# Splitting the normed input into two tiles, so that the last gate frees half of it in its middle and the attention output is loaded there

## The chip, the cores and the metric

The kernel runs on one core of one Trainium2 chip. It is written as one program of instructions for five engines (TensorE, VectorE, ScalarE, GpSimdE and SyncE; in the profile PE, DVE, ACT, POOL and SP), which wait for each other through semaphores. The metric is the device time of one launch in microseconds (us), median over runs. PEld is the weight load of PE, and SPq is SP's queue of transfers.

## The reference

One layer of a trunk with two branches over 640 tokens: 512 noisy tokens of one request and 128 context tokens. In short:

```python
h = _rmsnorm(x, p["norm1_g"]) * (1.0 + sc1) + sh1
u_rw, u_na, gate_rw, gate_na = jnp.split(h @ p["w_in"], IN_SPLITS, axis=-1)
o_rw, s_new = _rwkv_branch(u_rw, s0, ...)      # 8 heads, a scan forward and one backward
q, k, v = jnp.split(u_na, 3, axis=-1)          # 8 heads of attention in a 2-D neighbourhood
o_na = _na_latent(q, k, v, ctx_k, ctx_v, p["na_rpb"])
merged = (jax.nn.sigmoid(gate_rw) * (o_rw @ p["w_o_rwkv"])
          + jax.nn.sigmoid(gate_na) * (o_na @ p["w_o_na"]))
x = x + g1 * (merged @ p["w_out"])
h2 = _rmsnorm(x, p["norm2_g"]) * (1.0 + sc2) + sh2
x = x + g2 * ((jax.nn.silu(h2 @ p["ffn_w1"]) * (h2 @ p["ffn_w3"])) @ p["ffn_w2"])
```

d_model is 1024, each branch is 512 wide, the hidden layer of the feed-forward is 2816 wide. All is float32.

## The kernel before

**Two halves of every float32.** A matmul operand x is held as hi (x rounded to the type that PE multiplies at full rate) and lo (x minus hi). A product is three matmuls: hi by hi, hi by lo and lo by hi. The normed input h is held so, features on partitions: two tiles of 128 partitions by 8 feature blocks by 640 tokens (`hh` and `hl`, made by `hilo`, L314). `o`, the output of both branches, goes over the same two buffers once h is no longer read: `hilo("o")` asks for the same tags, and so each load of `o` waits for the last matmul that read the old content.

**The stages.** First the norm and q, k, v; then the attention, block by block; then four rounds (ct = 0 to 3, two heads each) of the other branch; then `w_out`, the second norm and the feed-forward. In a round, `inv` inverts 32 by 32 triangular blocks by a substitution in 30 steps on DVE (products into `pr`, L1249, and sums into `RL`, L1253), `carry` runs the chunked scan, `out` (L1385) normalises the round's result. In `inv`, three jobs of small matmuls (`v_job`, `t_job`, `g_job`: L1172, L1195, L1144, L1147, L1184) are issued after steps 2, 11 and 16 of the last round, and their results are masked on DVE after steps 4, 13 and 19 (L1156, L1159). The `out` of the round before runs beside `inv`; its matmuls are L1064, L1078 (five transposes) and L1407 (the gate, in two halves), and its DVE work L1398, L1399, L1402 and L1409 (two halves).

**The fill.** Between these instructions stands other dense work of PE, in the order of `PRM["order"]`: projections (k, r, v, l), sixteen gate blocks g0 to g15 (`gate_gen`, L534: sigmoid(gate) as a tanh, 24 matmuls for the first 320 tokens, a tanh on ACT, then 24 for the other 320, each result stored to `tna_d` or `trw_d`), and from a0 on the products of `o` with the output weights (`merge_gen`, L1450: a0 to a7 read o's blocks 0 to 3, the attention output; b0 to b7 read 4 to 6). g14 is the last gate, and a0 follows it. `flps` gives the fill two PSUM banks (`fl`) in turn.

**What sets the order.** PE, POOL, DVE and ACT execute in the order in which the code is written. `PRM["plan"]` gives for each step of the current stage how many matmuls of the fill, how many steps of `out` and how many of `bonus` (L1093, L1095) are written there. `later` puts an evacuation some steps behind its matmul. SP's transfers stand in an order of the scheduler's. `o_load(0, 6)` (L768) is written at the end of g14: twelve transfers of 320 KB, hi and lo of o's blocks 0 to 5; block 6 comes later.

Of the kernel before, what the change touches and what calls it, by code (L numbers as in the profile page):

```python
# [26 lines left out]
PRM = dict(  # L27
    order=("l0 l1 k0 r0 v0 l2 g0 g1 g2 k1 g3 r1 g4 g5 v1 g6 g7 k2 r2 g8 g9 v2 g10 g11 k3 r3 g12 g13 v3 g15 g14 a0 a1 a2 a3 a4 a5 a6 a7 "
     "b0 b1 b2 b4 b3 b5 b6 b7"),
    plan=(  # L30
        "22.0 0.0 2.0 4.0",
        ("0.0.0 2.0.0 2.0.1 10.0.0 2.0.0 2.0.1 2.0.1 2.0.1 2.0.1 2.0.1 10.0.0 2.0.0 2.0.0 10.0.0 2.0.0 2.0.0 "
         "2.0.0 10.0.0 2.0.0 2.0.0 2.0.0 2.0.0 2.0.0 2.0.0 2.0.0 2.0.0 2.0.0 2.0.0 2.0.0 2.0.0 5.0.0 24.0.0 "
         "20.0.0 10.0.0 8.0.0 8.0.0 0.0.0"),
        ("10.0 1.0 12.1 0.2 0.0 8.1 6.2 0.0 8.1 6.2 0.0 8.1 12.2 0.0 8.1 6.2 0.0 8.1 6.2 0.0 7.1 5.2 0.0 9.1 "
         "6.2 6.0"),
        "22.0 2.0 2.0 2.0",
        ("0.0.0 0.0.0 2.0.1 10.0.0 1.0.0 2.1.1 2.1.1 2.1.1 2.1.1 1.1.1 10.0.0 3.0.0 2.0.0 2.0.0 2.1.0 2.1.0 "
         "2.0.0 10.0.0 2.0.0 2.1.0 2.1.0 2.1.0 2.1.0 2.1.0 12.1.0 2.1.0 2.1.0 2.1.0 2.0.0 2.1.0 5.0.0 24.0.0 "
         "20.0.0 10.0.0 8.0.0 8.0.0 0.0.0"),  # L40
        ("10.0 0.0 8.1 6.2 0.0 8.1 6.2 0.0 8.1 6.2 0.0 8.1 6.2 0.0 8.1 6.2 0.0 7.1 6.2 0.0 8.1 6.2 0.0 8.1 "
         "6.2 6.0"),
        "22.0 2.0 0.0 5.0",
        ("0.0.0 10.0.0 2.0.1 10.0.0 2.0.0 2.1.1 2.1.1 2.1.2 2.1.1 2.1.0 10.0.0 2.0.0 2.0.0 2.0.0 2.1.0 2.1.0 "
         "2.0.0 10.0.0 2.0.0 2.1.0 2.1.0 3.1.0 4.1.0 2.1.0 2.1.0 2.1.0 2.1.0 4.1.0 2.1.0 2.0.0 5.0.0 24.0.0 "
         "18.0.0 8.0.0 9.0.0 8.0.0 0.0.0"),
        ("10.0 0.0 8.1 14.2 0.0 8.1 6.2 0.0 8.1 6.2 0.0 0.1 6.2 0.0 8.1 6.2 0.0 8.1 6.2 0.0 8.1 6.2 0.0 8.1 "
         "6.2 6.0"),
        "22.2 0.0 4.0 6.0",
        ("0.0.0 16.1.0 8.1.1 9.0.0 2.1.0 8.1.1 8.1.1 8.1.1 8.1.1 0.1.1 0.1.0 0.0.0 0.1.0 0.1.0 0.1.0 0.1.0 "  # L50
         "6.1.0 7.1.0 6.1.0 6.0.0 6.0.0 6.0.0 0.0.0 6.0.0 6.0.0 7.0.0 6.0.0 6.0.0 6.0.0 6.0.0 6.0.0 6.0.0 "
         "11.0.0 8.0.0 8.0.0 2.0.0 0.0.0"),
        ("10.0 0.0 8.1 6.2 0.0 8.1 4.2 0.0 8.1 6.2 0.0 8.1 6.2 0.0 8.1 6.2 0.0 8.1 6.2 0.0 8.1 6.2 0.0 8.1 "
         "14.2 6.0"),
        "2 0 6 6 6 4 4 5 2 0 5 1 1 0 0"),
    qp=((0, 0, 7, 6, 7), (2, 5, 4, 4, 3, 2, 5, 3, 1)), ada=2, pa=1, pd=0,
    lw=(0, 0, 0, 0, 0, 2, 2, 2, 2, 2, 2, 2, 2, 2, 2, 2),
# [50 lines left out]
def body(ctx: ExitStack, tc: tile.TileContext, xs, xp, cols, consts, w_ada, b_row, w_rw, w_qkv,  # L108
# [425 lines left out]
    def gate_gen(i, w, ps_, gsb, gtag):  # L534
        dst = trw_d[i] if i < 8 else tna_d[i - 8]
        for (a, b) in ((0, H2), (H2, NT)):
            t = gsb.tile([P, H2 if gtag == "fl" else 643], F32, tag=gtag, bufs=2, name=nm(gtag))[:, :H2]
            ps = ps_()
            yield from feat_gen(ps, w, (hh, hl), 8, a, b)

            def rest(t=t, ps=ps, a=a, b=b):
                act.activation(t, ps[:, :H2], AF.Tanh, scale=0.5)
                sp.dma_start(dst[:, a:b], t)
# [489 lines left out]
    with ExitStack() as s3:  # L1033
# [393 lines left out]
        def o_load(a, b):  # L1427

            if not o:
                o.extend(hilo("o"))  # L1430
            for q in range(a, b):
                for t, t_d in zip(o, o_d):
                    sp.dma_start(t.bitcast(F32)[:, q, :], t_d[q])
# [562 lines left out]
```

## Time and profile before

| what | us |
|---|---|
| median of 3 runs | 1203.76 |
| lowest and highest run | 1202.25 and 1204.63 |
| the profiled execution | 1201.55 |
| its span, first to last instruction | 1199.8 |
| PE busy in the span | 1128.0 |
| DVE busy in the span | 793.3 |
| ACT busy in the span | 503.6 |
| POOL busy in the span | 273.8 |

A row of a timeline gives the start in us from the span's start, the length in us, engine, line, operation, output <- inputs, shapes, a count, and in brackets the idle time of the engine ahead of it with what ended it. A row of the waits gives who waited <- for whom, us in total, times, and the longest. A row of the windows gives the stretch, its length, then for PE, PEld, DVE, ACT and POOL the busy time with the count, the granted PE clock as a share of full speed, the busy share of the DMA engines and GB/s.

### The profile page before, as it was taken

Reading aid. Unit: us, or ns where it says so; the run is one execution under the profiler, and the core shown is the slowest. Engines: PE = TensorE matmul, PEld = TensorE weight load, DVE = VectorE, ACT = ScalarE, POOL = GpSimd, SP = SyncE. Lnnn points to the kernel's source line nnn. Section 1 sums busy time; section 2 is a strip of 40 time slices with the busy share of each in tenths; the row PEclk is TensorE's granted clock in tenths of the full one; section 3 lists DMA queues with packets and bytes.
Section 4 is the critical chain, followed back from the end, with each engine's and each line's share of the span. In section 5 each row is a group of like instructions: output and inputs, shape, how many; then the busy total and the mean of one; then the engine's idle time right before and its main releaser. Section 6 shows DMA issues by size and latency. Waiting matters only on the chain.

```text
span 1199.8 us, 26920 instructions
## 1 busy us (share of the span) xinstructions
PE 1128.0 (94%) x11160; PEld 999.2 (83%) x11160; DVE 793.3 (66%) x1630; ACT 503.6 (42%) x1016; POOL 273.8 (23%) x354
## 2 busy tenths in 40 slices
PE   6999999998998899899789989989999999999998
PEld 4588877788887788788778878889889989998997
DVE  4565455569558838946594684888568756875675
ACT  4444666653454364346323331754224412442240
POOL 1162244343224323342231360200001000000000
PEclk9999999999899999999899989999999999999999
DMA  9752777531211221120432571312312231222122
GB/s 336 245 115 88 238 219 231 197 124 48 66 48 37 83 69 49 54 87 29 164 129 87 177 272 54 105 36 89 106 53 88 89 105 53 89 90 90 67 73 104
DMA packets 56578, 134.48 MB, mean 112 GB/s; under 512 B 7140, under 2 KB 22116, under 8 KB 56456
## 3 DMA queue, kind: packets, MB, share of 16 engines
q1 hardware_dynamic: 55592, 131.56, 33.1%
q8 instruction: 88, 1.44, 0.5%
q10 hardware_dynamic: 864, 1.20, 0.3%
q14 instruction: 34, 0.28, 0.1%
HBM read 118.41 MB, written 14.32 MB: 111 GB/s over the span
## 4 chain that ended last, share of the span: by engine, by line
PE 61%; DVE 11%; issue 2%; ACT 2%; DMA 1%; SPq 0%; POOL 0%; DVEq 0%; ACTq 0%
PE f L1715 23%; PE acc L283 16%; PE fl L196 10%; DVE pr L1249 2%; DVE RL L1253 2%; PE w L1361 1%; PE w L1321 1%; DVE AG L1104 1%; PE w L1333 1%; PE w L1348 1%; PE mm L196 1%; PE w L1147 1%; DMA tr<-trw_d 1%; PE w L1378 1%; DVE f L1262 1%
## 5 line engine op out<-in xcount | busy, mean ns | idle before, releaser
L196 PE MATMUL fl<-h,whi 128*128 128x320 f32 x704 | 170.4, 323 | 1.9 <-ACT U L515 1.0
L175 POOL TENSOR_TENSOR wlo<-wst,whi 128x256 fp32r<-128x256 f32 x118 | 102.8, 899 | 192.1 <-ACT whi L170 188.7
L1715 PE MATMUL f<-t,whi 128*128 128x320 f32 x640 | 141.4, 309 | 0.0
L1715 PE MATMUL f<-b,whi 128*128 128x320 f32 x608 | 136.4, 312 | 3.6 <-ACT b L185 1.8
L283 PE MATMUL acc<-whi,u 128*128 128x512 f32 (+1 forms) x448 | 135.9, 385 | 0.0
L196 PEld LDWEIGHTS fl<-h,whi 128*128 128x128 f32 x704 | 121.1, 192 | 6.8 <-ACT U L515 1.2
L170 ACT CAST whi<-wst 128x1024 fp32r<-128x1024 f32 (+2 forms) x86 | 81.8, 956 | 83.2 <-PE acc L283 32.9
L196 PE MATMUL fl<-h,wlo 128*128 128x320 f32 x352 | 114.6, 326 | 0.0
L1715 PEld LDWEIGHTS f<-t,whi 128*128 128x128 f32 x640 | 107.0, 188 | 0.0
L1715 PEld LDWEIGHTS f<-b,whi 128*128 128x128 f32 x608 | 102.8, 190 | 4.7 <-ACT b L185 2.2
L1770 POOL TENSOR_TENSOR ws<-wst 128x512 f32<-128x512 f32 x20 | 27.4, 1372 | 342.0 <-DVE wlo L1759 226.2
L1715 PE MATMUL f<-t,wlo 128*128 128x320 f32 x320 | 98.9, 309 | 0.0
L283 PEld LDWEIGHTS acc<-whi,u 128*128 128x128 f32 x448 | 83.5, 188 | 16.6
L1715 PE MATMUL f<-b,wlo 128*128 128x320 f32 x304 | 94.6, 311 | 1.4 <-DVE wlo L1759 1.4
L1756 ACT CAST whi<-ws 128x1024 fp32r<-128x1024 f32 x40 | 42.0, 1050 | 108.7 <-PE f L1715 48.5
L283 PE MATMUL acc<-wlo,u 128*128 128x512 f32 (+1 forms) x224 | 86.3, 385 | 0.0
L175 DVE TENSOR_TENSOR wlo<-wst,whi 128x1024 fp32r<-128x1024 f32 (+1 forms) x49 | 61.6, 1267 | 36.5 <-ACT whi L170 36.0
L283 PE MATMUL acc<-whi,h 128*128 128x512 f32 x240 | 78.7, 402 | 1.4 <-DVE h L397 1.4
L196 PEld LDWEIGHTS fl<-h,wlo 128*128 128x128 f32 x352 | 67.8, 193 | 2.6
L1555 DVE SCALAR_TENSOR_TENSOR tt<-acc,G 128x512 f32<-128x512 f32 (+1 forms) x51 | 34.7, 681 | 51.0 <-PE acc L283 51.0
L196 PE MATMUL mm<-h,whi 128*128 128x320 f32 x288 | 65.5, 315 | 0.0
L196 PE MATMUL fl<-o,whi 128*128 128x320 f32 x224 | 56.3, 331 | 7.1 <-DMA o<-o_d 4.8
(332 smaller groups left out, 2562.1 us busy)
## 6 DMA issues: line engine op xcount, KB each, us to landing
wst<-in_w_dram SPq DMA_DIRECT2D x66, 512.0 KB
wst<-in_w_rw_dram SPq DMA_DIRECT2D x31, 512.0 KB
wa<-in_w_ada_dram SPq DMA_DIRECT2D x24, 512.0 KB
f<-in_w_ada_dram SPq DMA_DIRECT2D x16, 512.0 KB
wst<-in_w_qkv_dram SPq DMA_DIRECT2D x12, 512.0 KB
o<-o_d SPq DMA_DIRECT2D x14, 320.0 KB
x<-in_xs_dram SPq DMA_DIRECT2D x8, 512.0 KB
wa<-in_w_ada_dram SPq DMA_DIRECT2D x16, 256.0 KB
```

The source lines that it names most:

```text
L170: act.copy(hi[:, :n], st[:, :n])
L175: eng.tensor_tensor(out=lo[:, a:b], in0=st[:, a:b], in1=hi[:, a:b].bitcast(F32), op=ALU.subtract)
L196: pe.matmul(ps[:, :t1 - t0], w[:, a:a + 128], x[:, k0 + kt, t0:t1], start=n == 0, stop=n == 3 * nk - 1)
L283: pe.matmul(pss[i][:, a:b], lhs(x, kt, ts_), w[:, cs_], start=ki == 0 and n == 0, stop=ki == last and n == 2)
L1104: dve.tensor_tensor(out=AG[rr, c, h, :], in0=c64(S.kk[rr, :], d), in1=S.P65[d][rr, :, 0:64], op=ALU.mult)
L1147: pe.matmul(pr[h][hrows[h ^ i], o_], x[hrows[h], :], R_[hrows[h], l, :], start=True, stop=True)
L1249: dve.tensor_tensor(out=prv, in0=V(RL[:, s + 1 + a, :], [[32, b - a], [0, s]], s), in1=V(RL[:, s, :], [[0, b - a], [1, s]]), op=ALU.mult)
L1253: dve.tensor_tensor(out=dst, in0=dst, in1=prv, op=ALU.add)
L1555: dve.scalar_tensor_tensor(out=tt, in0=ps[:, a:b], scalar=c, in1=G[:, g, sl], op0=ALU.mult, op1=ALU.mult)
L1715: pe.matmul(ps[:, :H2], w_[:, c_], x_[:, kt, :], start=first and kt + n == 0, stop=last and kt == 3 and n == 2, skip_group_check=more)
L1756: act.copy(r[0][:, :width], src())
L1770: eng_x(PRM["se"][i - 1]).tensor_tensor(out=o_, in0=x, in1=y, op=op)
```

## The change

The two tiles of h become four: `hilo` returns for hi and lo a small class `Two` over a tile for blocks 0 to 3 and one for blocks 4 to 7. All reads and writes of h, o and the later user `m` go through it. The gate g14 alone (`lg=14`) is computed by a new generator, `gate2_gen`: it goes through the feature blocks in pairs, and for each pair through both halves of the tokens, so both PSUM banks are open from its seventh matmul on. After its 24th matmul blocks 0 to 3 of h are read for the last time, and `o_load(0, 4)` is written there: eight of the twelve transfers. `o_load(4, 6)` stays at its end. Both tanh stand behind its 48th matmul. In the plan of the last round's `inv` the eleven steps "8 8 8 8 0 0 0 0 0 0 0" (matmuls of the fill per step) become "8 13 0 0 0 0 3 3 3 2 0". The other plan rows are only wrapped differently.

```diff
         "22.2 0.0 4.0 6.0",
-        ("0.0.0 16.1.0 8.1.1 9.0.0 2.1.0 8.1.1 8.1.1 8.1.1 8.1.1 0.1.1 0.1.0 0.0.0 0.1.0 0.1.0 0.1.0 0.1.0 "
...
+        ("0.0.0 16.1.0 8.1.1 9.0.0 2.1.0 8.1.1 13.1.1 0.1.1 0.1.1 0.1.1 0.1.0 3.0.0 3.1.0 3.1.0 2.1.0 "
+         "0.1.0 6.1.0 7.1.0 6.1.0 6.0.0 6.0.0 6.0.0 0.0.0 6.0.0 6.0.0 7.0.0 6.0.0 6.0.0 6.0.0 6.0.0 "
...
+    def hp_t(n, i, j):
+        return hp.tile([P, 4, NT], F32R, tag=f"hp{i}{j}", bufs=1, name=f"{n}{i}{j}")
+
+    class Two:
+
+        def __init__(self, ts):
+            self.ts = ts
+
+        def __getitem__(self, x):
+            return self.ts[x[1] // 4][x[0], x[1] % 4, x[2]]
+
     def hilo(n):
-        return [hp.tile([P, 8, NT], F32R, tag=f"hp{i}", bufs=1, name=f"{n}{i}") for i in range(2)]
+        return [Two([hp_t(n, i, j) for j in range(2)]) for i in range(2)]
...
+    def gate2_gen(i, w, ps_, gsb, gtag):
+        dst = trw_d[i] if i < 8 else tna_d[i - 8]
+        ps = [ps_(), None]
+        for kts in ((0, 1), (2, 3), (4, 5), (6, 7)):
+            for hf, (a, b) in enumerate(halves):
+                if ps[hf] is None:
+                    ps[hf] = ps_()
+                for kt in kts:
+                    for n, (u, x) in enumerate(((w[0], hh), (w[0], hl), (w[1], hh))):
+                        pe.matmul(ps[hf][:, :H2], u[:, kt * 128:kt * 128 + 128], x[:, kt, a:b],
+                                  start=kt == 0 and n == 0, stop=kt == 7 and n == 2)
+                        yield
+            if kts[1] == 3:
+                o_load(0, 4)
+
+        def rest(hf, a, b):
+            t = gsb.tile([P, H2 if gtag == "fl" else 643], F32, tag=gtag, bufs=2, name=nm(gtag))[:, :H2]
+            act.activation(t, ps[hf][:, :H2], AF.Tanh, scale=0.5)
+            sp.dma_start(dst[:, a:b], t)
+
+        for hf, (a, b) in enumerate(halves):
+            later(lambda hf=hf, a=a, b=b: rest(hf, a, b))
...
-                        o_load(0, 6)
+                        o_load(4, 6)
...
             if not o:
-                o.extend(hilo("o"))
+                o.extend(Two([]) for _ in range(2))
             for q in range(a, b):
-                for t, t_d in zip(o, o_d):
-                    sp.dma_start(t.bitcast(F32)[:, q, :], t_d[q])
+                for i, (t, t_d) in enumerate(zip(o, o_d)):
+                    if len(t.ts) == q // 4:
+                        t.ts.append(hp_t("o", i, q // 4))
+                    sp.dma_start(t[:, q, :].bitcast(F32), t_d[q])
```

Three places show what moves. The first is the start of g14 on PE (numbers behind a name tell buffers apart: `fl_7590` and `fl_7641` are the two banks of g14 before, `fl_7591` and `fl_7608` after; `h_89` to `h_92` are tiles of h). Before, from the sixth to the eighth matmul of g14 and at the change of its bank:

```order
L196 MATMUL fl_7590<-h_89,wlo_7430 128x320
L196 MATMUL fl_7590<-h_89,whi_7429 128x320
L196 MATMUL fl_7590<-h_90,whi_7429 128x320
...
L196 MATMUL fl_7590<-h_89,wlo_7430 128x320
L196 MATMUL fl_7641<-h_89,whi_7429 128x320
```

After, from the sixth matmul to the eighth:

```order
L567 MATMUL fl_7591<-h_89,whi_7431 128x320
L567 MATMUL fl_7591<-h_91,whi_7431 128x320
L567 MATMUL fl_7591<-h_89,wlo_7432 128x320
L567 MATMUL fl_7608<-h_89,whi_7431 128x320
L567 MATMUL fl_7608<-h_91,whi_7431 128x320
```

The second bank is now opened at the seventh matmul, where before it was opened at the 25th. The second place is SP's queue, before, from the transfer of weights for a2 (`wst`) on (`o_d_81` and `o_d_80` are the lo and hi halves in memory):

```order
L163 DMA wst_7812<-in_w_o_dram 128x512
L543 DMA tna_d<-fl_7589 128x320
L1433 DMA o_7799<-o_d_81 128x640 x2
L1433 DMA o_7798<-o_d_80 128x640 x3
L1433 DMA o_7799<-o_d_81 128x640
```

After:

```order
L163 DMA wst_7812<-in_w_o_dram 128x512
L1469 DMA o_7644<-o_d_81 128x640
L1469 DMA o_7642<-o_d_80 128x640 x2
L1469 DMA o_7644<-o_d_81 128x640
L1469 DMA o_7642<-o_d_80 128x640
```

The eight loads of o's blocks 0 to 3 stand right behind that weight, and the store of g14's first half is behind them. The third place is PE at the end of g14. Before, a0's seventh matmul, the transposes of `out`, and the rows ahead of the second job (L1195):

```order
L196 MATMUL fl_7815<-o_7798,whi_7610 128x320
L1078 MATMUL w_7832<-K,pre_7480 128x128 x4
L1078 MATMUL w_7833<-K,pre_7480 128x128
L196 MATMUL fl_7815<-o_7799,whi_7610 128x320
...
L1093 MATMUL w_7856<-bv_7361,K 128x320
...
L1407 MATMUL w_7877<-lg__618,gup_4523 128x320
L1195 MATMUL w_7895<-K,f_998_7387 64x64
```

After, where L1112, L1127, L1441 and L1229 are the lines L1078, L1093, L1407 and L1195 of before:

```order
L196 MATMUL fl_7815<-o_7642,wlo_7613 128x320
L1112 MATMUL w_7841<-K,pre_7482 128x128 x4
L1112 MATMUL w_7842<-K,pre_7482 128x128
L1127 MATMUL w_7856<-bv_7363,K 128x320
L1441 MATMUL w_7868<-lg__620,gup_4525 128x320
L196 MATMUL fl_7882<-o_7642,whi_7612 128x320
L196 MATMUL fl_7882<-o_7644,whi_7612 128x320
L196 MATMUL fl_7882<-o_7642,wlo_7613 128x320
L1229 MATMUL w_7890<-K,f_998_7389 64x64
```

The transposes stood behind 7 matmuls of a0 and stand behind 12, and the second job stood behind 23 and stands behind 15; the eight are issued behind that job, three of them ahead of L1407's second half.

More of the change, by code (lines that the diff above doesn't have):

```diff
@@ L49 @@
-        "22.2 0.0 4.0 6.0",
-        ("0.0.0 16.1.0 8.1.1 9.0.0 2.1.0 8.1.1 8.1.1 8.1.1 8.1.1 0.1.1 0.1.0 0.0.0 0.1.0 0.1.0 0.1.0 0.1.0 "
[L51 to L54, printed above, removed]
+        ("0.0.0 2.0.0 2.0.1 10.0.0 2.0.0 2.0.1 2.0.1 2.0.1 2.0.1 2.0.1 10.0.0 2.0.0 2.0.0 10.0.0 2.0.0 "
+         "2.0.0 2.0.0 10.0.0 2.0.0 2.0.0 2.0.0 2.0.0 2.0.0 2.0.0 2.0.0 2.0.0 2.0.0 2.0.0 2.0.0 2.0.0 "
+         "5.0.0 24.0.0 20.0.0 10.0.0 8.0.0 8.0.0 0.0.0"),
@@ new lines @@
+        ("10.0 1.0 12.1 0.2 0.0 8.1 6.2 0.0 8.1 6.2 0.0 8.1 12.2 0.0 8.1 6.2 0.0 8.1 6.2 0.0 7.1 5.2 "
+         "0.0 9.1 6.2 6.0"),
+        "22.0 2.0 2.0 2.0",
+        ("0.0.0 0.0.0 2.0.1 10.0.0 1.0.0 2.1.1 2.1.1 2.1.1 2.1.1 1.1.1 10.0.0 3.0.0 2.0.0 2.0.0 2.1.0 "
+         "2.1.0 2.0.0 10.0.0 2.0.0 2.1.0 2.1.0 2.1.0 2.1.0 2.1.0 12.1.0 2.1.0 2.1.0 2.1.0 2.0.0 2.1.0 "
+         "5.0.0 24.0.0 20.0.0 10.0.0 8.0.0 8.0.0 0.0.0"),
+        ("10.0 0.0 8.1 6.2 0.0 8.1 6.2 0.0 8.1 6.2 0.0 8.1 6.2 0.0 8.1 6.2 0.0 7.1 6.2 0.0 8.1 6.2 0.0 "
+         "8.1 6.2 6.0"),
@@ new lines @@
+        "22.0 2.0 0.0 5.0",
+        ("0.0.0 10.0.0 2.0.1 10.0.0 2.0.0 2.1.1 2.1.1 2.1.2 2.1.1 2.1.0 10.0.0 2.0.0 2.0.0 2.0.0 2.1.0 "
+         "2.1.0 2.0.0 10.0.0 2.0.0 2.1.0 2.1.0 3.1.0 4.1.0 2.1.0 2.1.0 2.1.0 2.1.0 4.1.0 2.1.0 2.0.0 "
+         "5.0.0 24.0.0 18.0.0 8.0.0 9.0.0 8.0.0 0.0.0"),
+        ("10.0 0.0 8.1 14.2 0.0 8.1 6.2 0.0 8.1 6.2 0.0 0.1 6.2 0.0 8.1 6.2 0.0 8.1 6.2 0.0 8.1 6.2 "
+         "0.0 8.1 6.2 6.0"),
+        "22.2 0.0 4.0 6.0",
+        ("0.0.0 16.1.0 8.1.1 9.0.0 2.1.0 8.1.1 13.1.1 0.1.1 0.1.1 0.1.1 0.1.0 3.0.0 3.1.0 3.1.0 2.1.0 "
+         "0.1.0 6.1.0 7.1.0 6.1.0 6.0.0 6.0.0 6.0.0 0.0.0 6.0.0 6.0.0 7.0.0 6.0.0 6.0.0 6.0.0 6.0.0 "
+         "6.0.0 6.0.0 11.0.0 8.0.0 8.0.0 2.0.0 0.0.0"),
@@ L55 @@
+        ("10.0 0.0 8.1 6.2 0.0 8.1 4.2 0.0 8.1 6.2 0.0 8.1 6.2 0.0 8.1 6.2 0.0 8.1 6.2 0.0 8.1 6.2 0.0 "
+         "8.1 14.2 6.0"),
         "2 0 6 6 6 4 4 5 2 0 5 1 1 0 0"),
@@ L73 @@
     h4=1.07, g1=2, km="dddddddd", kb="ddpd", ma="d", yo="pppp", r0="pd", rl=(0, 0, 0), lh=(0, 0, 1, 1),
-    wl="dddddddddppppppppppppppppppppppppppdpppppppppppp", nu=9, na=(
+    wl="dddddddddppppppppppppppppppppppppppdpppppppppppp", nu=9, lg=14, na=(
         "6.0.12.0.1 6.0.12.0.0 6.0.12.0.0 6.0.12.0.2 6.0.12.0.0 6.0.12.0.2 6.0.12.0.0 6.0.12.0.2 6.0.12.0.0 "
@@ L726, in unit @@
             return 48, lambda: wdma(w_rw[15 + i]), lambda w: wcast(w, eng), \
-                lambda w: gate_gen(i, w, flps, sb, gtag[-1])
+                lambda w: (gate2_gen if i == PRM["lg"] else gate_gen)(i, w, flps, sb, gtag[-1])
         ci, dst = {"k": (4 + i, kt_), "r": (i, rt_), "v": (8 + i, vp0), "l": (12 + i, lg_)}[g[0]]
```

15 lines of the change are left out of this document (removed).

## The prediction

> **What bounds the kernel now.** I read the page first: busy shares, then the chain that ended last.
>
> ```profile
> PE 1128.0 (94%) x11160; PEld 999.2 (83%) x11160; DVE 793.3 (66%) x1630; ACT 503.6 (42%) x1016; POOL 273.8 (23%) x354
> PE 61%; DVE 11%; issue 2%; ACT 2%; DMA 1%; SPq 0%; POOL 0%; DVEq 0%; ACTq 0%
> ```
>
> PE is idle for 1199.8 - 1128.0 = 72 us in all, so a change that removes no work can win only where PE, or an engine that the chain runs through, waits. "DMA 1%" of the chain is the place of this change. Next I read the waits between 570 and 625 us:
>
> ```profile
> DVE out L1398 <- PE w L1078: 7.3, 1, 7.3
> PE fl L196 <- DMA o<-o_d: 4.8, 1, 4.8
> DVE out L1409 <- PE w L1407: 2.2, 1, 2.2
> ```
>
> PE waits 4.8 us for the load of o, and DVE 7.3 us for the transposes (L1078) that stand in PE's queue behind it. The timelines of SP, PE and DVE show how:
>
> ```profile
> 579.66 0.33 SPq L163 DMA_DIRECT2D wst<-in_w_o_dram  x1
> 580.09 0.38 SPq L543 DMA_DIRECT2D tna_d<-fl  x1
> 586.97 6.80 SPq L1433 DMA_DIRECT2D o<-o_d  x12
> ...
> 587.07 0.55 PE L196 MATMUL fl<-h,wlo 128*128 128x320 f32 x1
> 592.40 0.90 PE L196 MATMUL fl<-o,whi 128*128 128x320 f32 x2 [4.78 <-DMA o<-o_d]
> 594.75 1.27 PE L1078 MATMUL w<-K,pre 128*128 128x128 f32 x5
> 595.67 0.61 PE L196 MATMUL fl<-o,whi 128*128 128x320 f32 x1
> 596.35 0.95 PE L196 MATMUL fl<-o,whi 128*128 128x320 f32 x2
> 597.10 0.38 PE L196 MATMUL fl<-o,wlo 128*128 128x320 f32 x1
> ...
> 588.21 0.38 DVE L1253 TENSOR_TENSOR RL<-RL,pr 128x72 f32<-128x72 f32 x2
> 595.85 0.69 DVE L1398 TENSOR_TENSOR out<-out,w 128x512 f32<-128x512 f32 x1 [7.25 <-PE w L1078]
> 597.92 0.82 DVE L1402 TENSOR_TENSOR out<-out,bv 128x640 f32<-128x640 f32 x1
> 600.43 0.48 DVE L1409 TENSOR_TENSOR out<-w,out 128x320 f32<-128x320 f32 x1
> 602.64 0.47 DVE L1253 TENSOR_TENSOR RL<-RL,pr 128x108 f32<-128x108 f32 x2
> 605.35 0.49 DVE L1409 TENSOR_TENSOR out<-w,out 128x320 f32<-128x320 f32 x1 [2.24 <-PE w L1407]
> ```
>
> SP starts the twelve loads at 586.97, when g14's last matmuls are under way. PE finishes g14 at 587.07 + 0.55 = 587.62 and gets o's block 0 at 592.40; the last pair of block 3 (596.35, x2) begins its second matmul about 0.27 before the next row, at 596.8. That is 596.8 - 586.97 = 9.8 us from the first issue to the last of the eight loads that a0 needs. DVE runs from 595.85 to 628 with only one gap over 1 us, the 2.24 at 605.35, so here the end is set by when DVE gets L1398, and then by when it gets the second L1409. The wait also cools PE's clock:
>
> ```profile
> 587.62:590.40 2.78, 0.01 (x1) 0.00 (x0) 0.97 (x5) 0.94 (x2) 1.40 (x2) 1.00 0.85 270
> 590.40:597.20 6.80, 4.80 (x17) 4.15 (x18) 1.35 (x6) 0.43 (x1) 0.00 (x0) 0.50 0.99 359
> 597.20:600.00 2.80, 2.80 (x17) 2.29 (x15) 2.65 (x11) 0.49 (x1) 0.00 (x0) 0.99 0.99 387
> ```
>
> The granted clock is 0.50 from 590.40 to 597.20 (third number from the right), 2.8 us after the wait began.
>
> **The change, part by part.** The span of the profiled execution is 1199.8, its time 1201.55, and the median of the runs 1203.76, so 2.2 above it; the terms are differences and I take them off the median.
>
> (1) *Two banks at once: costs 1.0 us of PE, hidden.* g14's seventh matmul now opens the second bank, which g15's second tanh has to empty first. In the trace g14 begins at 573.94, so its seventh matmul is at 574.82, and that tanh is late:
>
> ```profile
> 573.94 0.46 PE L196 MATMUL fl<-h,whi 128*128 128x320 f32 x2
> 574.82 0.46 PE L196 MATMUL fl<-h,whi 128*128 128x320 f32 x2
> ...
> 572.69 2.82 ACT L1130 COPY Nt<-w 128x512 f32<-128x512 f32 x4 [2.42 <-PE w L1125]
> 575.27 0.51 ACT L542 ACTIVATE fl<-fl 128x320 f32<-128x320 f32 x1
> ```
>
> It ends at 575.27 + 0.51 = 575.78, behind ACT's copies, so PE loses 575.8 - 574.8 = 1.0. Everything behind it in PE's queue is 1.0 later: L1064, the first job, g14's end (588.6), the masks that DVE does at 583.88. DVE is then free for L1398 at 589.6 instead of 588.6. What hides this is part (2): a0 waits for o longer than that. If o came at once, the 1.0 would count.
>
> (2) *Loads of o from the middle: gain.* SP may issue once the 24th matmul is done, about 578.6 + 1.0, but it first sits at the weight's transfer (579.66), which waits for POOL. The loads take the place of the store at 580.09: 6.88 earlier than now. Ahead of them in the engines is that weight, 256 KB, at the 387 GB/s above 0.7 us. So block 3 is complete between 596.8 - 6.88 = 589.9 (weight hidden) and 590.6 (weight in full); I take 590.6, because the loads saturate the DMA engines (share 0.99). PE alone, from 588.6 with 11 matmuls at 0.147 (twelve of them are 1.76), would need block 3's lo at 590.1. So a0 waits about 0.5 instead of 4.8, ends its first half at 590.6 + 0.3 = 590.9, and the transposes start there. Now they take 1.10 from their start to L1398 (594.75 to 595.85), of it 0.92 on PE at half clock; at full clock 0.46 + 0.18 = 0.64, at half clock 1.10. I take 0.75, near the warm end, since the wait before it is short. L1398 then starts at 591.65: **4.2 us earlier**. Bounds: 590.1 + 0.3 + 0.64 gives 4.8, and loads 1.5 us later than I say give 2.7. The store of g14's first half waits behind the loads; it is read by a6's load of the gate much later and costs nothing.
>
> (3) *The twelve matmuls ahead of the transposes instead of seven* are in (2). The first a0 evacuation on DVE (L1461, 0.41) goes to where DVE waits anyway; it is worth at most 0.2 ahead of L1402, because L1402 waits for ACT, which needs 0.92 after L1399. I count 0. So L1409's first half also comes 4.2 earlier, at 596.2.
>
> (4) *The second job comes too early now: a new wait.* PE has L1093, L1407, three matmuls of a0 and L1195 (1.1 us) behind the transposes and is at L1147 at about 593.7. But L1147 writes the bank that the first L1409 has to read, and that ends at 596.7. PE waits 3.0 us. It costs the chain nothing, as the job starts 4.2 earlier than now all the same:
>
> ```profile
> 600.09 1.16 PE L1195 MATMUL w<-K,f 64*64 64x64 f32 x64
> 603.89 0.27 PE L1184 MATMUL w<-ZV,J 64*64 64x64 f32 x1 [1.14 <-issue]
> 604.51 0.81 PE L1407 MATMUL w<-lg__618,gup 128*128 128x320 f32 x2
> ```
>
> Today the job runs from L1147 at 601.2 to 604.5 with a gap of 1.14 in which PE waited for nothing but its own instructions ("issue"). I leave that gap; it may vanish into the new wait (-1.1) or stay. Behind the job three matmuls of a0 stand ahead of L1407's second half: 3 x 0.147 = **+0.44**.
>
> (5) *Cold clock after the wait of (4).* The trace shows how little idle time lowers the clock:
>
> ```profile
> 686.00:689.40 3.40, 1.68 (x11) 1.19 (x10) 3.37 (x6) 1.40 (x2) 1.51 (x2) 1.00 0.48 154
> 689.40:692.80 3.40, 2.90 (x11) 2.50 (x11) 3.40 (x9) 0.71 (x2) 0.17 (x1) 0.50 0.45 160
> 302.30:303.74 1.44, 1.42 (x81) 1.38 (x81) 1.34 (x3) 0.00 (x0) 0.00 (x0) 0.50 0.00 0
> 627.94:629.34 1.40, 1.40 (x80) 1.35 (x80) 1.40 (x3) 0.00 (x0) 0.89 (x2) 1.00 0.04 12
> ```
>
> A stretch in which PE was busy for 1.68 of 3.40 is followed by one at 0.50. So 3.0 of idle will most likely be followed by it too. It does not slow small matmuls: the 80 of L1273 take 1.44 at half clock and 1.40 at full clock. It slows the three of a0: 17 matmuls at half clock in 4.80 - 0.92 give about 0.27 each against 0.147, so 3 x 0.12 = **+0.36** on the chain. By the Trainium skill, page "TensorE: Matmul & The Clock Gate", section "What's actually happening", the clock falls only after an idle window of about 3.4 us; by that it would stay warm and the gain be 0.36 larger, but the row above fell with half that idle time, and I go by the row.
>
> Sum at the second L1409: 4.2 - 0.44 - 0.36 = 3.4 us earlier. From there DVE has no gap that could swallow it, PE's five more matmuls (0.7 to 1.3) end where job three waits for DVE's masks, and the rest of the round, the feed-forward too, hang on this chain and not on a clock. So 1203.76 - 3.4 = **1200.4** (and 1198.2 for an execution like the profiled one).
>
> **The rivals.** *More:* the 1.14 of issue vanishes into the wait of (4) and the clock stays up: 3.4 + 1.1 + 0.36 = 4.9, 1198.9. Speaking for it: PE's queue stands still for 3 us. Against: the gap belongs to a place in the instruction stream, which the change shifts by only 8 matmuls.
>
> *Less:* the loads of o run beside the weight, the dense first job and PE's instruction fetch, and are 1 to 2.5 us slower. Each us counts from the first, as PE has only 0.5 to spare: 1201.4 to 1202.9, say 1202.2. Against it: SP issues the same eight in the same way, and nothing else moves much in that window (the store is gone).
>
> *Slower:* PE starves for instructions. In the first job PE already lost time to it, and the burst now falls there:
>
> ```profile
> 582.99 0.21 PE L1147 MATMUL w<-R__2889,f 64*64 64x64 f32 x1 [0.49 <-issue]
> q8 instruction: 88, 1.44, 0.5%
> 100.00:200.00 100.00, 97.41 (x724) 78.57 (x724) 49.52 (x126) 56.50 (x141) 31.87 (x50) 1.00 0.65 211
> ```
>
> A packet of instructions is 1.44 MB / 88 = 16 KB. If it had to wait until the eight loads are in (590.6), the 0.49 would grow to about 8, g14 would end at 596, and L1398 would come at 598.7: 2.9 late, 1206.7. It decides from a stall of about 6 us (cover of part 2, 0.5, plus the gain) on. Against it: from 100 to 200 us the DMA engines are 0.65 busy and PE idles 2.6 of 100; but only 724 matmuls run there. The Trainium skill, page "DMA: Bandwidth & Descriptors", section "Queues, rings and completion order", says that each engine takes turns between queues, packet by packet, which would hold such a fetch up only briefly; no run here shows it yet.
>
> *No effect:* SP does not issue earlier, or something later in the round sets the end: 1203.5.
>
> **How the numbers follow.** 0.2% (2.4 us, from 1201.35 to 1206.2) is about what a measurement of this kernel can tell from no change. Chances: the forecast (1199.0 to 1201.4) 0.56; more 0.14; less 0.17; slower 0.08; no effect 0.05. Faster therefore 0.56 + 0.14 = 0.70, and of "less" nearly all falls within 0.2%: 0.21 with "no effect"; slower 0.09. The range takes in "more" and "less" with the runs' spread of about 1 us: 1198.0 to 1203.4.
>
> **What would show it.** SP's loads of o in two groups, the first at about 580.1; a PE wait of about 1 us for ACT at g14's seventh matmul; a wait for o under 1 us; L1398 about 4 us earlier; a PE wait of about 3 us for DVE in front of L1147 and a half-clock stretch behind it; DVE's second L1409 3 to 4 us earlier. I am wrong if o's block 3 arrives after 592, if the issue gaps in the first job exceed 1 us, or if the shift is there at 605 and gone by 690.

## The result and the profile after

The changed kernel takes 1200.08 us (median of 15 executions, from 1196.71 to 1205.03) against 1203.76 before (15 executions, from 1200.61 to 1206.51). The ratio is 0.9969 with a 95% interval of 0.9955 to 0.9983, so 0.31% faster; 1200.4 had been forecast. The profiled execution took 1200.39, with a span of 1198.5.

The page of the changed kernel, its busy row and its chain by engine:

```profile
PE 1132.9 (95%) x11160; PEld 1004.7 (84%) x11160; DVE 792.7 (66%) x1630; ACT 503.6 (42%) x1016; POOL 273.7 (23%) x354
PE 60%; DVE 13%; ACT 2%; issue 2%; DMA 1%; SPq 0%; POOL 0%; DVEq 0%; ACTq 0%
```

They look like those of before: 4.9 us more of busy PE in a shorter span. What moved is seen only in the stage. The timelines of SP, PE, DVE of the changed kernel, at the places that the prediction named:

```profile
581.07 0.33 SPq L163 DMA_DIRECT2D wst<-in_w_o_dram  x1
581.78 4.88 SPq L1469 DMA_DIRECT2D o<-o_d  x8
591.73 1.82 SPq L1469 DMA_DIRECT2D o<-o_d  x4
...
577.87 0.55 PE L567 MATMUL fl<-h,whi 128*128 128x320 f32 x2 [0.85 <-ACT fl L553]
587.60 0.21 PE L1181 MATMUL w<-R__2891,f 64*64 64x64 f32 x1 [1.95 <-issue]
592.08 0.46 PE L196 MATMUL fl<-o,whi 128*128 128x320 f32 x2
593.84 0.71 PE L1112 MATMUL w<-K,pre 128*128 128x128 f32 x5
597.63 0.33 PE L1181 MATMUL w<-R__2891,f 64*64 64x64 f32 x2 [0.35 <-DVE bv L1129]
599.40 0.28 PE L1181 MATMUL w<-R__2891,f 64*64 64x64 f32 x3 [1.45 <-DVE out L1443]
...
594.48 0.69 DVE L1432 TENSOR_TENSOR out<-out,w 128x512 f32<-128x512 f32 x1 [1.27 <-PE w L1112]
598.87 0.48 DVE L1443 TENSOR_TENSOR out<-w,out 128x320 f32<-128x320 f32 x1
604.11 0.49 DVE L1443 TENSOR_TENSOR out<-w,out 128x320 f32<-128x320 f32 x1 [1.90 <-PE w L1441]
```

SP issues eight loads right behind the weight, PE waits 0.85 for g15's tanh, a0 begins at 592.08 without any wait for o, and DVE waits 1.27 for the transposes where it waited 7.25. (L1098, L1112, L1181, L1218, L1432, L1441 and L1443 are L1064, L1078, L1147, L1184, L1398, L1407 and L1409 of before.)

One thing must be taken out before the two profiles are compared: g14's first matmul is at 573.94 before and at 575.98 after. These 2.04 us arose ahead of the change; the run `before2` below shows that they come and go with the same program. All distances from here on are therefore counted from g14's first matmul, each as a difference of two rows of a timeline. The table has every profile of this study, the runs of the next section included; "issue gap" is PE's idle time in the first job that the profile puts down to "issue", and the last column goes to the start of the last instruction.

| kernel | g14 starts | issue gap | L1398 / L1432 | second L1409 / L1443 | last |
|---|---|---|---|---|---|
| before | 573.94 | 0.49 | 21.91 | 31.41 | 625.8 |
| before2 (the same) | 576.90 | 0.60 | 23.00 | 32.55 | 628.5 |
| after | 575.98 | 1.95 | 18.50 | 28.13 | 622.5 |
| loadline (the same rows) | 577.71 | 1.56 | 18.11 | 27.74 | 622.2 |
| after_b (the same) | 576.77 | 1.56 | 18.11 | 27.75 | 622.3 |
| split | 575.51 | 0.49 | 20.23 | 30.29 | 625.0 |
| swap | 581.51 | 1.01 | 26.86 | 35.71 | 629.1 |
| noload | 575.02 | 0.57 | 17.12 | 25.46 | 618.9 |
| oldplan, oldplan_b | 579.74, 578.66 | 0.77, 1.59 | 16.58, 17.39 | 25.53, 26.06 | 621.6, 619.5 |
| wide, wide_b | 575.27, 574.16 | 1.98, 0.68 | 17.65, 17.12 | 27.30, 26.79 | 621.9, 621.7 |
| wide_oldplan, _b | 576.95, 572.74 | 2.64, 1.86 | 17.57, 16.79 | 25.83, 25.54 | 619.4, 619.0 |

Counted so, L1432 comes 3.41 us earlier than before, the second L1443 3.28 earlier, and the last instruction 3.3 earlier: what is won by the second L1443 reaches the end whole. Other profiles of the same two programs differ by about as much as 1 us here: over the two of before and the three of the changed program the second L1443 comes 3.28 to 4.81 earlier.

### The profile page after: what moved, and what is told of

Same layout as the page of the kernel before. It is cut to its first block, busy times and chain, and to the rows that moved or that the text cites. A ratio compares the mean times of both kernels' runs of the same rounds, so it can differ in the third digit from the quotient of the medians.

```text
span 1198.5 us, 26923 instructions
## 1 busy us (share of the span) xinstructions
PE 1132.9 (95%) x11160; PEld 1004.7 (84%) x11160; DVE 792.7 (66%) x1630; ACT 503.6 (42%) x1016; POOL 273.7 (23%) x354
## 3 DMA queue, kind: packets, MB, share of 16 engines
q8 instruction: 88, 1.44, 0.5%
## 4 chain that ended last, share of the span: by engine, by line
PE 60%; DVE 13%; ACT 2%; issue 2%; DMA 1%; SPq 0%; POOL 0%; DVEq 0%; ACTq 0%
PE f L1751 21%; PE acc L283 16%; PE fl L196 10%; DVE pr L1283 2%; DVE RL L1287 2%; PE w L1355 1%; PE w L1395 1%; PE w L1382 1%; PE w L1367 1%; PE mm L196 1%; PE w L1181 1%; DVE AG L1138 1%; DMA tr<-trw_d 1%; PE w L1412 1%; DVE AG L1190 1%
## 5 line engine op out<-in xcount | busy, mean ns | idle before, releaser
L196 PE MATMUL fl<-h,whi 128*128 128x320 f32 x672 | 165.3, 328 | 2.0 <-ACT U L526 1.0
L196 PEld LDWEIGHTS fl<-h,whi 128*128 128x128 f32 x672 | 117.6, 196 | 7.2 <-ACT U L526 1.6
L196 PE MATMUL fl<-h,wlo 128*128 128x320 f32 x336 | 110.6, 329 | 0.0
L283 PEld LDWEIGHTS acc<-whi,u 128*128 128x128 f32 x448 | 83.5, 188 | 16.7
L1407 DVE TENSOR_TENSOR ZV<-w,Dt 64x128 f32<-64x128 f32 x64 | 18.5, 288 | 67.0 <-PE w L1395 65.9
```

The source lines that it names most:

```text
L196: pe.matmul(ps[:, :t1 - t0], w[:, a:a + 128], x[:, k0 + kt, t0:t1], start=n == 0, stop=n == 3 * nk - 1)
L283: pe.matmul(pss[i][:, a:b], lhs(x, kt, ts_), w[:, cs_], start=ki == 0 and n == 0, stop=ki == last and n == 2)
L1407: dve.tensor_tensor(out=V(ZV[own, l + 1, h, :], [[128 * dl, 2], [1, 64]]), in0=V(pn[own, :], [[64, 2], [1, 64]], 64 * g), in1=V(Dt[own, 0, ...
```

## The experiments

**Is it the early load?** In `swap` the only edit puts o's two groups of blocks over the other group's buffers, so that the large load has to wait for g14's end:

```diff
-                        t.ts.append(hp_t("o", i, q // 4))
+                        t.ts.append(hp_t("o", i, 1 - q // 4))
```

> The changed kernel, but o's blocks 0 to 3 go over the buffers of h's blocks 4 to 7 and blocks 4 and 5 over those of h's blocks 0 to 3: the same order of matmuls, the same plan, and the large load cannot start before g14 ends. Distances are counted from g14's first matmul to the start of DVE's second L1409 (L1443 here): 31.4 us before the change, 28.1 after it. Theory (the gain is the early load): the eight loads start at about 15 us, behind the store of g14's first half, block 3 is in at 25, and since the transposes now stand behind twelve matmuls of a0, L1432 comes at about 26 (18.5 in the changed kernel) and the second L1443 at 35.5 to 36. Time 1207.5 to 1208.5. Rival (the gain is the new plan or the order of the matmuls): the distance stays at 28 to 29 and the time at 1200 to 1201.

Measured: 1211.05 us, ratio to before 1.006 (1.0039 to 1.0081). SP, PE and DVE of `swap`:

```profile
587.31 1.74 SPq L1469 DMA_DIRECT2D o<-o_d  x4
596.32 3.94 SPq L1469 DMA_DIRECT2D o<-o_d  x8
...
600.15 0.53 PE L196 MATMUL fl<-o,whi 128*128 128x320 f32 x2 [3.32 <-DMA o<-o_d]
603.39 0.63 PE L196 MATMUL fl<-o,whi 128*128 128x320 f32 x1 [1.20 <-DMA o<-o_d]
...
608.37 0.69 DVE L1432 TENSOR_TENSOR out<-out,w 128x512 f32<-128x512 f32 x1 [10.57 <-PE w L1112]
617.22 0.49 DVE L1443 TENSOR_TENSOR out<-w,out 128x320 f32<-128x320 f32 x1 [1.12 <-PE w L1441]
```

The eight loads start 596.32 - 581.51 = 14.8 us after g14's first matmul (13.0 in the kernel before), PE waits for o again, and the second L1443 comes at 35.71, in the forecast's 35.5 to 36. With the order of the matmuls and the plan of the changed kernel but a late load, the kernel is slower than before: these two give nothing without the early load. The time is 2.5 us above the forecast's 1208.5. From g14 on the kernel takes 6.6 us more than the changed one, which would make 1206.7. The other 4 of its time lie ahead of g14, which starts at 581.51 here, 5.5 later than in the changed kernel's profile; whether the clock alone (last section) did that in its executions is open.

**Is it the place of the line?** `loadline` writes the load where it stood before, at g14's end:

```diff
-            if kts[1] == 3:
-                o_load(0, 4)
...
-                        o_load(4, 6)
+                        o_load(0, 6)
```

> The changed kernel with the load of blocks 0 to 3 written at g14's end, together with blocks 4 and 5, instead of in its middle. SP's transfers stand in the scheduler's order, and here each engine's rows are the same as in the changed kernel. Theory (the split tile and the order of g14's matmuls free the buffers, the scheduler does the rest): nothing changes, SP's first load comes 5.8 us after g14's first matmul, time 1200.1 within the noise of about 1; and since the program is the same, the differences between the two profiles show what one execution is worth: the issue gap in the first job anywhere from 0.5 to 2 us, the half clock in the second job there or not, the second L1443 at 25.5 to 28.2. Rival (the place of the line matters): the loads start at 13 to 15 us, and the time is 1206 or more.

Measured: 1201.32 us, ratio 0.9975 (0.9961 to 0.9989). SP of `loadline`, whose lines are two lower here:

```profile
582.79 0.33 SPq L163 DMA_DIRECT2D wst<-in_w_o_dram  x1
583.50 4.62 SPq L1467 DMA_DIRECT2D o<-o_d  x8
```

The first load comes 583.50 - 577.71 = 5.79 us after g14's first matmul, as in the changed kernel (581.78 - 575.98 = 5.80). Each engine's rows are the same in both programs. "o loads from the gate's middle on" is thus not the work of the line that says so: it follows from which tile is free when, and the scheduler finds the place.

**Is the split of the tile enough?** `split` is the kernel before with only the tiles of h split: g14 in the old order, the old plan.

```diff
-        ("0.0.0 16.1.0 8.1.1 9.0.0 2.1.0 8.1.1 13.1.1 0.1.1 0.1.1 0.1.1 0.1.0 3.0.0 3.1.0 3.1.0 2.1.0 "
+        ("0.0.0 16.1.0 8.1.1 9.0.0 2.1.0 8.1.1 8.1.1 8.1.1 8.1.1 0.1.1 0.1.0 0.0.0 0.1.0 0.1.0 0.1.0 "
...
-    wl="dddddddddppppppppppppppppppppppppppdpppppppppppp", nu=9, lg=14, na=(
+    wl="dddddddddppppppppppppppppppppppppppdpppppppppppp", nu=9, lg=-1, na=(
...
-                        o_load(4, 6)
+                        o_load(0, 6)
```

> The kernel before with only the tiles of h split in two: g14 in its old order (one half of the tokens after the other), the old plan, o loaded at its end. Blocks 0 to 3 of h are then read last by g14's 36th matmul, 11.1 us after its first. Theory (the gain goes with the time at which the loads start): they start at 11.3 instead of 13.0, a0 starts at 16.7 instead of 18.5, L1398 comes at 20.2 instead of 21.9 and the second L1409 at 29.7 instead of 31.4; time 1202.0. Rival 1 (the split is enough for the whole gain): 28 or less and 1200.5. Rival 2 (the loads start no earlier, as SP's queue holds them): 31.4 and 1203.8.

Measured: 1202.82 us, ratio 0.9991 (0.9977 to 1.0005), no difference that can be told. SP, PE and DVE of `split`:

```profile
586.79 6.95 SPq L1469 DMA_DIRECT2D o<-o_d  x12
...
590.82 0.56 PE L196 MATMUL fl<-o,whi 128*128 128x320 f32 x2 [1.61 <-DMA o<-o_d]
592.10 0.63 PE L196 MATMUL fl<-o,whi 128*128 128x320 f32 x1 [0.58 <-DMA o<-o_d]
593.44 0.63 PE L196 MATMUL fl<-o,whi 128*128 128x320 f32 x1 [0.71 <-DMA o<-o_d]
...
595.75 0.69 DVE L1432 TENSOR_TENSOR out<-out,w 128x512 f32<-128x512 f32 x1 [5.58 <-PE w L1112]
605.80 0.49 DVE L1443 TENSOR_TENSOR out<-w,out 128x320 f32<-128x320 f32 x1 [2.12 <-PE w L1441]
```

The loads start at 586.79 - 575.51 = 11.3 and L1432 comes at 20.2, both as forecast. The second L1443 comes at 30.3, where 29.7 had been forecast, and the last instruction 0.8 earlier than in `before`. PE still waits for o in three places, 1.61 + 0.58 + 0.71 = 2.9 us. The split gives 1.7 of the 3.4 us at L1432; the other half needs g14's order, which frees blocks 0 to 3 at the 24th matmul instead of the 36th.

**What does the load itself cost?** `noload` leaves the eight loads out, so that a0 to a7 take their first four blocks from h:

```diff
-                        t.ts.append(hp_t("o", i, q // 4))
+                        t.ts.append(hp_t("o", i, 1) if q // 4 else (hh, hl)[i].ts[0])
+                    if q < 4:
+                        continue
                     sp.dma_start(t[:, q, :].bitcast(F32), t_d[q])
```

> The changed kernel without the eight loads of o's blocks 0 to 3: a0 to a7 read blocks 0 to 3 of h in their place, so a part of the result is left out. It shows what the load itself costs. Theory (the loads hold up PE's instructions in the first job): PE's issue gap of 1.95 us in L1181 goes back to about 0.5, as before the change, L1432 comes at 17.0 us from g14's first matmul instead of 18.5, and the second L1443 at 26.7 instead of 28.1; time 1198.7. Rival (the gap belongs to the place in the stream of instructions, or differs from one execution to the next): a gap of 1.5 or more stays, and 28.1; time 1200.1.

Measured: 1197.64 us, ratio 0.9945 (0.9927 to 0.9963). PE and DVE of `noload`:

```profile
585.25 0.21 PE L1181 MATMUL w<-R__2891,f 64*64 64x64 f32 x1 [0.57 <-issue]
597.06 0.28 PE L1181 MATMUL w<-R__2891,f 64*64 64x64 f32 x3 [1.44 <-DVE out L1443]
...
592.14 0.69 DVE L1432 TENSOR_TENSOR out<-out,w 128x512 f32<-128x512 f32 x1 [1.27 <-PE w L1112]
600.48 0.49 DVE L1443 TENSOR_TENSOR out<-w,out 128x320 f32<-128x320 f32 x1 [0.61 <-PE w L1441]
```

The issue gap is 0.57 instead of 1.95, and L1432 comes at 17.12, as forecast. In the table the gap is 0.49 to 0.60 in the four profiles with no load of o in the first job, 1.01 in `swap` with four of them there, and 0.68 to 2.64, mean 1.62, in the nine with eight. So the burst does hold up PE's instructions, by about 1.1 us on average and by a different amount in each execution.

"Issue" names no cause, but the packets of the instruction queue (q8) in the same traces point to one. Two windows of 0.1 us, of the kernel before (580.6 to 580.7) and of the changed one (585.3 to 585.4), each hold the start of one such packet of 16 KB; its time, as a share of 16 engines, makes 0.93 and 0.96 us:

```profile
q8 instruction: 1, 0.02, 58.1%
q8 instruction: 1, 0.02, 60.0%
```

Counted from g14's first matmul, the packet runs from 6.73 to 7.66 before, from 7.55 to 8.94 in `noload` and from 9.35 to 10.31 in the changed kernel (the last two include 0.85 of the wait for the bank), and PE goes on at 9.05, 10.24 and 11.62. In all fourteen profiles the gap stands in front of the same matmul, 192 places behind g14's first, and ends 1.0 to 1.6 us after this packet has landed. So it is the fetch of instructions that is late: beside the loads its packet starts later and takes no longer (0.9 to 1.4 us with and without them). What it waits for before its start the traces do not show.

The second L1443 comes 1.2 earlier than forecast (25.46, not 26.7). The reason stands in the second job, from the end of its wait to its last matmul, first in the changed kernel and then in `noload`:

```profile
599.40:602.68 3.28, 3.28 (x118) 3.16 (x118) 2.81 (x13) 1.53 (x4) 1.60 (x1) 0.53 0.03 7
```

```profile
597.06:599.20 2.14, 2.14 (x119) 2.02 (x119) 2.14 (x10) 1.50 (x4) 1.60 (x1) 1.00 0.01 4
```

The same job behind the same wait takes 3.28 us in the changed kernel, nearly all of it at half clock (0.53), and 2.14 at full clock: 1.14 more.

**What does the new plan do?** `oldplan` is the changed kernel with the plan row of before.

```diff
-        ("0.0.0 16.1.0 8.1.1 9.0.0 2.1.0 8.1.1 13.1.1 0.1.1 0.1.1 0.1.1 0.1.0 3.0.0 3.1.0 3.1.0 2.1.0 "
+        ("0.0.0 16.1.0 8.1.1 9.0.0 2.1.0 8.1.1 8.1.1 8.1.1 8.1.1 0.1.1 0.1.0 0.0.0 0.1.0 0.1.0 0.1.0 "
```

> The changed kernel with the plan row of the kernel before. Theory (the plan gives nothing, it makes the second job come too early): the transposes stand behind 7 instead of 12 matmuls of a0, so L1432 comes 0.7 earlier (17.8 us from g14's first matmul instead of 18.5); the second job stands behind 23 instead of 15, so PE's wait of 1.8 in front of L1181 falls to under 0.5, the clock stays up in the job, and no matmul of a0 stands between the job and L1441. The second L1443 comes at 25.5 to 26.5 instead of 28.1; time 1197.6 to 1198.6. Rival (the plan is a part of the gain, because without it a0's later blocks or the second job hold up the transposes): 28.5 or more, time 1200.5 to 1202.

Measured: 1200.15 us, ratio 0.9973 (0.9961 to 0.9985). PE and DVE of `oldplan`:

```profile
590.18 0.21 PE L1181 MATMUL w<-R__2891,f 64*64 64x64 f32 x1 [0.77 <-issue]
601.30 0.28 PE L1181 MATMUL w<-R__2891,f 64*64 64x64 f32 x3 [0.17 <-DVE out L1443]
603.81 0.27 PE L1218 MATMUL w<-ZV,J 64*64 64x64 f32 x1 [0.90 <-issue]
...
605.27 0.49 DVE L1443 TENSOR_TENSOR out<-w,out 128x320 f32<-128x320 f32 x1 [1.83 <-PE w L1441]
```

The distance is what was forecast: PE waits 0.17 in front of the second job instead of 1.80 in two pieces, the clock stays up, and the second L1443 comes at 25.53 instead of 28.13. A part of this is chance, as the issue gap of the first job was 0.77 here and 1.95 there: L1432 came at 16.6 instead of the forecast's 17.8. The issue gap in the second job is back with 0.90. But the time is that of the changed kernel, where 1197.6 to 1198.6 had been forecast.

**What does the second bank cost?** `wide` goes through g14's blocks in groups of four, so that the second bank opens at the 13th matmul:

```diff
-        for kts in ((0, 1), (2, 3), (4, 5), (6, 7)):
+        for kts in ((0, 1, 2, 3), (4, 5, 6, 7)):
...
-            if kts[1] == 3:
+            if kts[0] == 0:
```

> The changed kernel with g14's feature blocks in groups of four instead of two, so that its second bank is opened at the 13th matmul instead of the 7th. Theory (the wait for g15's tanh is on the path now, since the load of o is not waited for any more): PE's wait of 0.85 goes to under 0.2, L1432 comes 0.7 to 0.8 earlier (17.7 us from g14's first matmul instead of 18.5), the second L1443 at 27.3; time 0.8 less, 1199.3. Rival (o's block 3 is what the transposes wait for): PE waits for o instead, the distance stays at 28.0 to 28.2 and the time at 1200.1.

Measured: 1199.09 us, ratio 0.9974 (0.9957 to 0.9991). PE and DVE of `wide`:

```profile
577.16 0.56 PE L567 MATMUL fl<-h,whi 128*128 128x320 f32 x2
586.03 0.21 PE L1181 MATMUL w<-R__2891,f 64*64 64x64 f32 x1 [1.98 <-issue]
...
602.57 0.49 DVE L1443 TENSOR_TENSOR out<-w,out 128x320 f32<-128x320 f32 x1 [1.91 <-PE w L1441]
```

The 13th matmul starts at 577.16 with no wait of the size of 0.85, and the second L1443 comes at 27.30 as forecast, with an issue gap (1.98) like the changed kernel's. So the wait for the tanh is on the path, 0.83 us of it. The time does not tell 0.8 us.

**Both together**, and the same program of before once more:

> Both earlier edits of the changed kernel together: g14's feature blocks in groups of four and the plan row of before. Theory: the 0.75 of the bank wait comes off on top of the old plan: second L1443 at 24.8 us from g14's first matmul (25.5 with the old plan alone, 27.3 with groups of four alone), with an issue gap of about 0.8 in the first job; time 1199.2. Rival (the old plan shows nothing in the times, as the median of that run says): 26.5 to 27.5, time as with groups of four alone, 1199.1 to 1200.1.

Measured: 1197.92 us, ratio 0.9948 (0.9931 to 0.9965). In its profile the second L1443 comes at 25.83 behind an issue gap of 2.64, where 24.8 behind a gap of 0.8 had been forecast; the longer gap alone is more than the difference.

> The kernel before, once more, for a second profile of the same program. Theory (the 2.0 us by which g14 starts later in the changed kernel's profile come from the clock's windows, not from the change): g14's first matmul at another time than 573.9, by up to 4 us, with another number of half-clock stretches ahead of it, and the distances behind it the same within 0.5: L1398 at 21.9, the second L1409 at 31.4. Rival (the change delays g14): 573.9 again.

Measured, one execution: 1207.22 us. PE and DVE of `before2`:

```profile
586.06 0.21 PE L1147 MATMUL w<-R__2889,f 64*64 64x64 f32 x1 [0.60 <-issue]
596.32 0.90 PE L196 MATMUL fl<-o,whi 128*128 128x320 f32 x2 [5.62 <-DMA o<-o_d]
...
609.45 0.49 DVE L1409 TENSOR_TENSOR out<-w,out 128x320 f32<-128x320 f32 x1 [2.48 <-PE w L1407]
```

g14 starts at 576.90 here and at 573.94 in the first profile of the same program, so the 2.04 between before and after says nothing about the change. The distances repeat less well than forecast: L1398 at 23.0 and the second L1409 at 32.55, 1.1 more, of it 0.85 in the wait for o (5.62 against 4.77).

**The four side by side.** The changed kernel, the two edits and both, timed together against the kernel before on one chip:

> The changed kernel once more, beside the three runs that follow, so that the four are compared on one chip. The distance from g14's first matmul to DVE's second L1443 was 28.1 and 27.7 us in the two profiles of this program, with issue gaps of 1.95 and 1.56 in the first job and the second job at half clock in both. Theory: 27 to 28.2 again (25.5 to 26.5 if the clock stays up in the second job); time 0.997 of before, 1200.5.

> The changed kernel with the plan row of before, once more. Its one profile gave 25.5 us to the second L1443, with an issue gap of 0.77; its median gave no gain over the changed kernel. Theory (the new plan costs, as it sends the second job into a wait and a half clock): 25.5 plus the issue gap's excess over 0.8, so 25.5 to 27.3, and a time 1 to 2 us under after_b. Rival (the plan is worth nothing either way): the distance stays under after_b's but the time is the same, and something later in the round gives the gain back at the same place, so that from the second L1443 to the end this kernel takes longer by as much.

> Groups of four feature blocks, new plan, once more. Its one profile gave 27.3 us with an issue gap of 1.98. Theory: 0.75 less than the changed kernel at the same issue gap, so 26.5 to 27.5; time 0.5 to 1 us under after_b. Rival: no difference in time.

> Groups of four and the old plan, once more. Its one profile gave 25.8 us with an issue gap of 2.64, and its median 1197.9. Theory: both edits count, the sum of the two differences: 24.0 to 26 us, and a time 2 to 3 us under after_b. Rival (the six runs of before were low by chance): a time like the lower of oldplan_b and wide_b.

| kernel | us | ratio to before | 95% interval |
|---|---|---|---|
| after_b | 1200.55 | 0.9974 | 0.9959 to 0.9988 |
| oldplan_b | 1200.07 | 0.9973 | 0.9957 to 0.9988 |
| wide_b | 1199.41 | 0.9973 | 0.9956 to 0.9990 |
| wide_oldplan_b | 1196.63 | 0.9945 | 0.9922 to 0.9968 |

PE and DVE of `wide_oldplan_b`:

```profile
583.39 0.21 PE L1181 MATMUL w<-R__2891,f 64*64 64x64 f32 x1 [1.86 <-issue]
594.52 0.28 PE L1181 MATMUL w<-R__2891,f 64*64 64x64 f32 x3 [0.18 <-DVE out L1443]
596.82 0.27 PE L1218 MATMUL w<-ZV,J 64*64 64x64 f32 x1 [0.70 <-issue]
...
598.28 0.49 DVE L1443 TENSOR_TENSOR out<-w,out 128x320 f32<-128x320 f32 x1 [1.63 <-PE w L1441]
```

The four distances lie in the forecast ranges. The times do so less well: the old plan alone is 0.5 us under after_b (1 to 2 forecast), groups of four alone 1.1 (0.5 to 1), and both together 3.9 (2 to 3). Both edits together give a kernel that is faster than the changed one: 0.9948 and 0.9945 of before in two comparisons, where the changed program had 0.9969, 0.9975 and 0.9974. Its distance to the end, 619.0 and 619.4, is 3 us under the changed kernel's, and its times are 3 to 4 us under. In `wide_b` the issue gap happened to be 0.68, and there PE waits for o again (0.30 at its longest): L1432 comes at the same 17.12 as in `noload` with its 0.57, although the bank wait is gone too.

Neither edit alone can be told from the changed kernel by its time, and why both together bring 3 to 4 us is open. So is the old plan with groups of two. Its two profiles end at 621.6 and 619.5, 0.7 and 2.8 under the changed kernel's mean of 622.3, and its two medians (1200.15 and 1200.07) show none of it beyond 0.5. The first profile lost 1.9 us against the second between 684 and 709, in the stage of `w_out`, where it had two half-clock stretches of 6.8 us and the second had one of 3.4. Whether the plan brings this on or chance does, two profiles do not tell.

## Why the prediction was right, and where it was not

It was right in sign and size, and in the mechanism that carries the gain, the early load: the forecast was 3.4 us at the second L1409, measured 3.28 from g14's first matmul, and 3.7 in the medians. Several of its steps were not right, and that the sum still came out so close is in part luck. One of its own signs of being wrong came true: the issue gap in the first job exceeded 1 us. Step by step:

(1) *The second bank.* Forecast a wait of 1.0, hidden by the wait for o. Measured 0.85. It is not hidden: `wide` shows 0.83 on the path. The step failed in its cover, because PE did not wait for o at all.

(2) *The load.* Start 5.8 us after g14's first matmul (6.15 forecast). The packets of the eight loads end at 591.51, 15.5 after g14's start (16.7 forecast): from the first issue to the end they took 9.7 us with the weight ahead of them, as the 9.8 of before, where the forecast had added 0.7 for it and a start 0.35 later. On the other side g14 ended 1.6 us later than forecast, at 16.26, of which 1.46 is the issue gap in the first job, grown from 0.49 to 1.95. That took the 0.5 of waiting for o away and more (588.6 + 11 x 0.147 is 590.2, so it was 0.4; the sum does not use it). L1398 moved by 3.41, not 4.2. The mis-sized term is the issue gap, which the sum left as it was. The prediction had it as the rival "slower", with a gap of 8 us if the fetch waited for the whole load; it exists, at about a fifth of that. By the Trainium skill, page "DMA: Bandwidth & Descriptors", section "Queues, rings and completion order", the engines take turns between queues packet by packet. The trace agrees in so far as the instruction packet landed at 10.31, over 5 us ahead of the last packet of the loads.

(3) *The a0 evacuation that moved.* Counted at 0; nothing in the rows contradicts it: from L1398 to the first L1409 it was 26.49 - 21.91 = 4.58 us before and 598.87 - 594.48 = 4.39 after.

(4) *The second job comes too early.* Forecast a wait of 3.0 for DVE in front of L1147; measured 0.35 (for L1129) and 1.45, 1.80 in all. PE came to the job 1.5 later than forecast (597.63 - 0.35 - 575.98 = 21.3 after g14's first matmul, not 593.7 - 573.94 = 19.8), and the first L1443 ended only 0.6 later. The issue gap of 1.14 in the job was left in the sum. It is gone: it passed during the wait, as the rival "more" had it. The six profiles with such a wait of 1.8 have no issue gap in this job, and the eight with a wait of 0.37 or less have one of 0.21 to 1.39, `swap` with the new plan among them (0.48). In the changed kernel the packet of instructions that this job lacked before landed at 23.25, while PE still waited (until 23.43); before it landed at 28.5, 1.25 after the job's L1147 had begun.

(5) *The cold clock.* Forecast on the row in which 1.7 us of idle time in 3.4 was followed by half clock. It came after 1.8 us. (The 0.27 of a matmul at half clock is right, by rows such as 596.09 and 596.35 of the kernel before; the division given for it makes 0.23.) But the forecast had it slow only three matmuls of a0, 0.36, and said small matmuls do not suffer, from the 80 of L1273 (1.44 against 1.40). Those of the job do: 3.28 against 2.14. This 1.14 too much and the 1.14 of (4) too little cancel, so that from the first to the second L1409 it was 605.35 - 600.43 = 4.92 before and 604.11 - 598.87 = 5.24 after: 0.32 lost, where 0.80 had been forecast.

So the sum was right partly because two errors of one size had opposite signs. The 0.8 that L1432 fell short was made up behind it, 0.2 in (3) and 0.5 in (4) and (5); that is luck. That DVE has no gap that could swallow the gain, and that the feed-forward hangs on this chain, held: 3.3 at the last instruction.

## What to carry to other kernels

A transfer that waits for the last reader of a large tile can be had earlier by splitting the tile and reading the half that is wanted first; the line in which the load is written did not matter here, the time at which its buffer is free did. When a wait goes, look again at what it hid: a wait for the bank and an issue gap cost nothing as long as PE waited 4.8 for o, and both were on the path afterwards. The better form of this change differs in two small edits, one of which takes the wait for the bank away. A plan that fills a wait should be looked at again when the wait is gone. Where a wait is put down to "issue", look when the packets of the instruction queue land.
